# State space preparation: the input matrices' scale ahead of the phase powers, the first C clearing ahead of the input matrices

## The chip, the cores and the metric

One core of a Trainium2 chip runs the whole program. The time is the device time of one execution in microseconds (us). Before the change it was 1484.26 us, the median of three runs (1483.49 to 1489.04).

## The reference

The reference is a small network for one sequence of 256 positions with 1024 channels, in float32. A first block has two layers; each is a mixer (gated linear attention, a short convolution and causal latent attention side by side) followed by a cross attention to 256 memory positions. A second block follows with feed-forwards, a state space mixer (S5) in its first layer and a sparse attention in its second.

The change touches what is computed from the state space mixer's parameters alone. For each of 64 groups with 64 states and 16 channels:

```python
dt = exp(log_dt); mag = exp(a_re * dt)
ab = mag * (cos(a_im * dt) + i sin(a_im * dt))      # one step's factor
z  = (ab - 1) / a                                    # scale of the input matrices
bb = z * b                                           # input matrices, complex
# bu = u @ bb;  state = ab * state + bu;  y = state @ c   along the sequence
```

The kernel treats four positions at once, so it also needs powers of ab, and a table of rotations (the phase of ab taken to 4, 8, 16 and so on) with which the recurrence is run.

## The kernel before, in words

Activations lie transposed, channels on the partitions. Each weight is split into a high part (a copy by ACT, L156) and a remainder (a subtraction by DVE, L157), and each product is three matmuls (L72 is the line of all matmuls, L76 that of all transposes). Weights arrive in halves of 512 KB through SP's queue into `raw`, and the parts into `hi` (three buffers) and `lo` (two). A projection of 256 columns is 48 matmuls of 128x256.

The framework orders the instructions of PE, ACT and DVE before the run, by the order in which the program gives them out and by when it thinks their inputs are ready; on the chip each engine then takes its list in order. POOL is an exception: its instructions are kept exactly in the order of the program (L60 is the line of all of them). Besides the state space work POOL computes the power -1/2 of each norm: `rx` in the cross attention, `rg` in the mixer, `rf` in the final norm.

The preparation `s5_prep` is a generator, and so is `s5_prep_tile`, which makes the records of one of eight tiles (`kt`). The main program calls `bg()` after most of its steps. `bg()` adds to an account a share of PE's time since the last call (0.4 in the first block, 0.7 in the feed-forwards, at most 10000 in all, by prices in the code) and runs the generator from `yield` to `yield` while the account is positive. A step costs POOL's time by the code's prices, but at least 1000. The preparation starts when the first layer's cross attention is about to begin; the tiles go on through the second layer and the first feed-forward. What is left is drained before the state space mixer.

The order of the preparation, as it stands:

- the parameters are loaded into a buffer with the tag `pcb` and transposed by PE; ACT and DVE compute mag, cos and sin, and the powers `pw` of ab;
- `E`: the phase squared over and over, six times, on DVE (44 small instructions with `r4`, in two steps);
- the scale z (`zr`, `zi`): 13 small instructions on DVE;
- `bb`: six products of 128x512 on POOL;
- then for each tile: clear the C tile, again with the tag `pcb` (one buffer); two products each for X0 and X1 from `bb` and `pw`, with sums into `pX`; PE transposes C and ACT copies it into `pcb` (L1256, L1257); POOL's products of C and `pw`; records transposed by PE, copied by ACT (L1279) and stored by POOL's queue; and last the rotation table from `E` on POOL.

In the cross attention (`cross`) the order is: values of the memory (`mem_v(0)`), first queries (`queries(0)`), the squares of hT and their sums (L350) for the norm, `rx`, second queries, scores (DVE's L865 to L872, ACT's L868), and the rest. The functions of the change, and what calls them:

Of the kernel before, what the change touches and what calls it, by code (L numbers as in the profile page):

```python
# [11 lines left out]
F32 = mybir.dt.float32  # L12
# [7 lines left out]
P = 128  # L20
# [8 lines left out]
MUL, ADD, SUB, MAX, MIN = ALU.mult, ALU.add, ALU.subtract, ALU.max, ALU.min  # L29
# [49 lines left out]
class Net:  # L79
# [1028 lines left out]
    def s5_prep(self):  # L1108
        nc, T = self.nc, self.T
        V, A, G, PE = nc.vector, nc.scalar, self.G, self.PE  # L1110
        H = 32
# [4 lines left out]
        v = {n: prm[:, i, :] for i, n in enumerate(names)}  # L1116
        pw = self.pz.tile([P, 2, 5, H], F32, name="pw", tag="pw", bufs=1)
# [15 lines left out]
        p = self.ps("pq")[:, :4 * H].rearrange("p (i q) -> p i q", i=4)  # L1133
# [4 lines left out]
        TT = lambda o, a, b, op: V.tensor_tensor(o, a, b, op=op)  # L1138
# [14 lines left out]

        def cmul(o, a, b, s, E=TT):
            E(o[0], a[0], b[0], MUL)
            E(s[0], a[1], b[1], MUL)
            E(o[1], a[0], b[1], MUL)
            E(s[1], a[1], b[0], MUL)
            E(o[0], o[0], s[0], SUB)
            E(o[1], o[1], s[1], ADD)  # L1160

        pwj = lambda j: (pw[:, 0, j, :], pw[:, 1, j, :])
        tmp = (v["t0"], v["t1"])
        for j, a, b in ((2, 1, 1), (3, 2, 1), (4, 2, 2)):
            cmul(pwj(j), pwj(a), pwj(b), tmp)
        u1, u2 = (v["cos"], v["sin"]), (v["u2r"], v["u2i"])
        cmul(u2, u1, u1, tmp)
        yield

        E = self.pz.tile([P, 6, 3, H], F32, name="E", tag="E", bufs=1)  # L1170
        cmul((E[:, 0, 0], E[:, 0, 2]), u2, u2, tmp)
        for k in range(6):
            if k:
                cmul((E[:, k, 0], E[:, k, 2]), *2 * ((E[:, k - 1, 0], E[:, k - 1, 2]),), tmp)
            V.tensor_scalar(E[:, k, 1], E[:, k, 2], -1.0, None, op0=MUL)
            if k == 3:
                yield
        self.r4 = self.const([P, H], "r4")
        TT(self.r4, v["mag"], v["mag"], MUL)
        TT(self.r4, self.r4, self.r4, MUL)  # L1180

        TT(v["t0"], v["are"], v["are"], MUL)
        TT(v["t1"], v["aim"], v["aim"], MUL)
        TT(v["t0"], v["t0"], v["t1"], ADD)
# [9 lines left out]
        TT(v["zi"], v["zi"], v["dt"], MUL)  # L1194
        yield

        bb = self.pz.tile([P, 2, 512], F32, name="bb", tag="bb", bufs=1)
        GT = lambda o, a, b, op: G.tensor_tensor(o, a, b, op=op)
        zb = [v[n][:, :, None].to_broadcast([P, H, 16]) for n in ("zr", "zi")]
# [2 lines left out]
        cmul([h16(bb[:, i, :]) for i in range(2)], [h16(t) for t in bn], zb,  # L1202
             [h16(s_) for s_ in sc], GT)
        yield
        for kt in range(KD):
            yield from self.s5_prep_tile(kt, v, pw, bb, E)

    def s5_c(self, kt):

# [5 lines left out]
                                       self.T[n][0, 8 * kt:8 * kt + 8].rearrange("g h p -> (g h) p")[:, None, :].to_broadcast([P, 2, 64]))  # L1215
                self.raws.append(raw)

    def s5_prep_tile(self, kt, v, pw, bb, E):
        nc, T = self.nc, self.T
        V, A, G, PE = nc.vector, nc.scalar, self.G, self.PE  # L1220
        dst = self.stash[kt]
# [5 lines left out]
        v4 = lambda t: t.rearrange("p (q i c) -> p q i c", q=4, i=4)  # L1227
        half = (slice(0, 64), slice(64, 128))
        raws = self.raws
        cb = self.pt("pcb", 1).rearrange("p (a q g h) -> p a q g h", a=4, q=4, g=2)  # L1230
        G.memset(cb[:, 0:2], 0.0)
        yield

        b4 = [bb[:, i, q0 * 16:(q0 + 4) * 16].rearrange("p (q h) -> p q h", h=16)[:, :, None, :].to_broadcast(qih)
              for i in range(2)]
# [14 lines left out]
        for c in range(2):  # L1250
            p = self.ps("pq")[:, :P]
            PE.transpose(p, raws[c], self.ident)
            p = p.rearrange("p (q g h) -> p q g h", q=4, g=2)
# [21 lines left out]
        for c in range(2):  # L1275
            p = self.ps("pq")
# [748 lines left out]
```

## Time and profile before

| what | us |
|---|---|
| median of three runs | 1484.26 |
| lowest, highest | 1483.49, 1489.04 |
| the profiled execution | 1480.56 |
| its span, first to last instruction | 1478.7 |
| PE busy | 1418.3 |
| DVE busy | 1010.4 |
| ACT busy | 749.0 |
| POOL busy | 296.5 |

The profile is of one execution. Busy is the time in which an engine had an instruction at work; the rest of the span it waited. PE's ends are modelled, so a busy PE need not be at its peak. The granted clock of PE is 1.00 at its higher level (2.4 GHz) and 0.50 at its lower (1.2 GHz). Times in the views count from the start of the span.

### The profile page before, as it was taken

How to read it: one execution, taken by the hardware profiler on the slowest of the kernel's cores; microseconds unless marked ns; L12 is line 12 of the kernel's file. 1: busy time of each engine (PE TensorE's matmuls, PEld its weight loads, DVE VectorE, ACT ScalarE, POOL GpSimd, SP SyncE). 2: the span in 40 equal slices, each digit the busy share in tenths (PEclk: the TensorE clock that was granted, in tenths of full speed). 3: DMA queues.
4: the chain of work that ended last, by engine and by line, in shares of the span. 5: the costliest groups of instructions: out<-in, count | busy, mean ns of one | idle time of the engine just before them, and what ended most of it. 6: DMA issues, size and time to landing. Idle time of an engine off the chain costs nothing.

```text
span 1478.7 us, 29034 instructions
## 1 busy us (share of the span) xinstructions
PE 1418.3 (96%) x11775; PEld 1326.5 (90%) x11775; DVE 1010.4 (68%) x1815; ACT 749.0 (51%) x1289; POOL 296.5 (20%) x421
## 2 busy tenths in 40 slices
PE   8899979999998999999899999999999989999998
PEld 6898968888988999989799999899999977899987
DVE  6867946887758887648866765566665478657654
ACT  6744555654555554432354444464444377644432
POOL 3000171652627888500000000011000010000000
PEclk9999999999999999996999999999999999999999
DMA  6653633554644766686446556756665631255653
GB/s 189 166 158 101 195 115 108 162 156 131 216 134 144 224 219 198 217 301 219 159 143 194 186 177 187 202 170 181 194 190 188 199 115 58 77 168 185 196 186 131
DMA packets 244296, 252.77 MB, mean 171 GB/s; under 512 B 31378, under 2 KB 226808, under 8 KB 243265
## 3 DMA queue, kind: packets, MB, share of 16 engines
q1 hardware_dynamic: 239408, 236.20, 51.4%
q0 software_dynamic: 4464, 14.63, 3.0%
q8 instruction: 93, 1.52, 0.4%
q14 instruction: 43, 0.34, 0.1%
q10 hardware_dynamic: 288, 0.07, 0.0%
HBM read 235.40 MB, written 15.47 MB: 170 GB/s over the span
## 4 chain that ended last, share of the span: by engine, by line
PE 43%; issue 10%; DVE 3%; POOL 1%; ACT 1%; DMA 0%; POOLq 0%; DVEq 0%; ACTq 0%
PE ps L72 39%; PE pb L72 2%; PE pq L72 1%; DVE lo L157 1%; POOL hq L60 0%; POOL pv L60 0%; DMA raw<-in_w_o_dram 0%; DVE rz L1468 0%; ACT hi L156 0%; POOL pt L60 0%; DVE hqm L1540 0%; PE po L72 0%; DVE ra L1467 0%; DVE s L1805 0%; DVE ra L1457 0%
## 5 line engine op out<-in xcount | busy, mean ns | idle before, releaser
L156 ACT ACTIVATE hi<-raw 128x1024 fp32r<-128x1024 f32 (+3 forms) x428 | 429.9, 1012 | 505.4 <-PE ps L72 198.3
L157 DVE TENSOR_TENSOR lo<-raw,hi 128x1024 fp32r<-128x1024 f32 (+3 forms) x428 | 507.8, 1203 | 104.2 <-issue 51.6
L72 PE MATMUL ps<-xh,hi 128*128 128x256 f32 x1848 | 523.7, 283 | 1.5 <-ACT xh L389 1.1
L72 PE MATMUL ps<-xh,lo 128*128 128x256 f32 x1848 | 520.5, 282 | 3.5 <-DVE lo L157 3.5
L72 PE MATMUL ps<-xl,hi 128*128 128x256 f32 x1848 | 520.8, 282 | 0.6 <-DVE xl L390 0.6
L72 PEld LDWEIGHTS ps<-xh,hi 128*128 128x128 f32 x1848 | 349.1, 189 | 10.2 <-issue 6.3
L72 PEld LDWEIGHTS ps<-xh,lo 128*128 128x128 f32 x1848 | 349.2, 189 | 5.8 <-DVE lo L157 4.2
L72 PEld LDWEIGHTS ps<-xl,hi 128*128 128x128 f32 x1848 | 349.2, 189 | 4.2 <-issue 2.5
L72 PE MATMUL ps<-gl,hi 128*128 128x256 f32 x576 | 162.6, 283 | 1.4 <-DVE gl L1488 1.4
L72 PE MATMUL ps<-gh,hi 128*128 128x256 f32 x576 | 161.7, 283 | 0.9 <-ACT gh L1487 0.9
L72 PE MATMUL ps<-gh,lo 128*128 128x256 f32 x576 | 162.1, 282 | 0.0
L72 PEld LDWEIGHTS ps<-gl,hi 128*128 128x128 f32 x576 | 109.4, 190 | 2.3 <-DVE gl L1488 1.6
L72 PEld LDWEIGHTS ps<-gh,hi 128*128 128x128 f32 x576 | 108.7, 190 | 2.1 <-ACT gh L1487 1.3
L72 PEld LDWEIGHTS ps<-gh,lo 128*128 128x128 f32 x576 | 109.4, 190 | 0.3
L1041 DVE TENSOR_TENSOR ab<-ps,rbf 128x512 f32<-128x512 f32 x66 | 45.6, 690 | 72.8 <-PE ps L72 67.4
L72 PE MATMUL ps<-L,hi 128*128 128x256 f32 (+1 forms) x384 | 72.9, 286 | 0.8 <-ACT L L887 0.8
L72 PEld LDWEIGHTS ps<-L,hi 128*128 128x128 f32 (+1 forms) x384 | 58.4, 182 | 2.0 <-ACT L L887 1.5
L72 PE MATMUL ps<-L,lo 128*128 128x256 f32 (+1 forms) x192 | 54.3, 284 | 1.4 <-DVE bc L732 1.4
L236 DVE TENSOR_TENSOR gl<-e,gh 128x512 fp32r<-128x512 f32 x44 | 32.3, 735 | 29.3 <-ACT gh L235 29.3
L60 POOL TENSOR_TENSOR rkvs<-rkvsa,mhalf 128x2 f32<-128x2 f32 x1 | 0.7, 697 | 190.2 <-DVE rkvsa L369 190.2
L1047 DVE SCALAR_TENSOR_TENSOR e<-e,ab 128x512 f32<-128x512 f32 x44 | 32.6, 741 | 7.4 <-ACT e L1046 7.2
L72 PEld LDWEIGHTS ps<-L,lo 128*128 128x128 f32 (+1 forms) x192 | 35.0, 182 | 2.2 <-DVE bc L732 1.7
(578 smaller groups left out, 2375.3 us busy)
## 6 DMA issues: line engine op xcount, KB each, us to landing
raw<-in_ffn_w_in_dram SPq DMA_DIRECT2D x176, 512.0 KB, 4.3
raw<-in_ffn_w_out_dram SPq DMA_DIRECT2D x68, 512.0 KB, 4.5
raw<-in_w_in_dram SPq DMA_DIRECT2D x24, 512.0 KB, 5.2
stash<-pv POOLq DMA_DIRECT2D x24, 512.0 KB, 4.2
raw<-in_ffn_w_out_dram SPq DMA_DIRECT2D x24, 384.0 KB, 3.5
raw<-in_w_out_dram SPq DMA_DIRECT2D x16, 512.0 KB, 4.2
raw<-in_w_in_dram SPq DMA_DIRECT2D x24, 256.0 KB, 3.4
rec<-stash SPq DMA_DIRECT2D x4, 1536.0 KB, 6.3
```

The source lines that it names most:

```text
L60: return self.tc.keep_in_program_order(f(out, *a, **k))
L72: return self.engine.matmul(out, w, x, **k)
L156: self.nc.scalar.activation(dst(h), src(raw), AF.Copy)
L157: (engine or self.nc.vector).tensor_tensor(dst(l), src(raw), dst(h).bitcast(F32), op=SUB)
L236: self.nc.vector.tensor_tensor(lo, src, hi.bitcast(F32), op=SUB)
L1041: V.tensor_tensor(v[-1], p, rb2, op=MUL)
L1047: V.scalar_tensor_tensor(th, th, 1.0, v[0], op0=ADD, op1=MUL)
```

## The change

Three things move. In `s5_prep` the 13 instructions of the scale come ahead of the phase powers `E` and `r4`. The first tile's C buffer is taken and cleared, by a new function `s5_cb`, before the products `bb` are given out, and handed to `s5_prep_tile`. The phase powers follow the products, in two steps with a `yield` behind them. For the other seven tiles the clearing stays at the head of the tile, but the `yield` behind it is gone, so that it forms one step with the first products.

```diff
@@ s5_prep @@
         cmul(u2, u1, u1, tmp)
         yield
-        E = ...; cmul(...); six squarings with a yield after the fourth; r4
         TT(v["t0"], v["are"], v["are"], MUL)
...
         TT(v["zi"], v["zi"], v["dt"], MUL)
         yield
+        cb = self.s5_cb()
         bb = self.pz.tile([P, 2, 512], F32, name="bb", tag="bb", bufs=1)
...
         yield
+        E = self.pz.tile([P, 6, 3, H], F32, name="E", tag="E", bufs=1)
+        cmul((E[:, 0, 0], E[:, 0, 2]), u2, u2, tmp)
+        for k in range(6):
+            if k:
+                cmul((E[:, k, 0], E[:, k, 2]), *2 * ((E[:, k - 1, 0], E[:, k - 1, 2]),), tmp)
+            V.tensor_scalar(E[:, k, 1], E[:, k, 2], -1.0, None, op0=MUL)
+            if k == 3:
+                yield
+        self.r4 = self.const([P, H], "r4")
+        TT(self.r4, v["mag"], v["mag"], MUL)
+        TT(self.r4, self.r4, self.r4, MUL)
+        yield
         for kt in range(KD):
-            yield from self.s5_prep_tile(kt, v, pw, bb, E)
+            yield from self.s5_prep_tile(kt, v, pw, bb, E, self.s5_cb() if kt else cb)

+    def s5_cb(self):
+        cb = self.pt("pcb", 1).rearrange("p (a q g h) -> p a q g h", a=4, q=4, g=2)
+        self.G.memset(cb[:, 0:2], 0.0)
+        return cb

@@ s5_prep_tile @@
-        cb = self.pt("pcb", 1).rearrange("p (a q g h) -> p a q g h", a=4, q=4, g=2)
-        G.memset(cb[:, 0:2], 0.0)
-        yield
```

## Rows read from the trace of the kernel before

**Rows 1.** The page, busy time and share of the span by engine.
```profile
PE 1418.3 (96%) x11775; PEld 1326.5 (90%) x11775; DVE 1010.4 (68%) x1815; ACT 749.0 (51%) x1289; POOL 296.5 (20%) x421
```
**Rows 2.** By stretch: length, busy PE, PEld, DVE, ACT, POOL, clock, DMA share, GB/s.
```profile
172.00:176.00 4.00, 4.00 (x36) 4.00 (x35) 4.00 (x19) 1.86 (x3) 0.00 (x0) 1.00 0.53 161
...
194.00:197.00 3.00, 3.00 (x15) 3.00 (x16) 0.00 (x0) 1.33 (x2) 2.80 (x5) 0.55 0.02 5
```
**Rows 3.** Timeline of POOL: start, us, engine, line, operation, idle time before.
```profile
180.63 1.06 POOL L60 TENSOR_TENSOR bb<-pX,prm 128x512 f32<-128x512 f32 x1 [49.78 <-DVE prm L1138]
...
189.48 0.31 POOL L60 MEMSET pcb<- 128x256 f32 x1
...
190.22 1.24 POOL L60 TENSOR_TENSOR pt<-bb,pw 128x256 f32<-128x256 f32 x2
...
198.94 1.52 POOL L60 TENSOR_TENSOR pv<-pt 64x256 f32<-64x256 f32 x2
200.54 0.71 POOL L60 TENSOR_TENSOR rx<-rxa,mhalf 128x2 f32<-128x2 f32 x1
```
**Rows 4.** Timeline of ACT, first layer's cross attention.
```profile
179.30 0.83 ACT L843 ACTIVATE qT<-ps,rm 128x256 f32<-128x256 f32 x2
...
189.82 0.22 ACT L1256 ACTIVATE pcb<-pq 64x64 f32<-64x64 f32 x1 [7.99 <-POOL pcb L60]
...
191.70 1.14 ACT L350 ACTIVATE sq<-hT 128x512 f32<-128x512 f32 x2
```
**Rows 5.** Timeline of PE, first layer's cross attention.
```profile
182.39 0.64 PE L72 MATMUL pb<-sq,ones 128*32 128x256 f32 x8
...
192.37 1.58 PE L72 MATMUL pb<-sq,ones 128*32 128x256 f32 x8 [7.73 <-ACT sq L350]
...
200.80 1.89 PE L72 MATMUL pb<-kT,L 128*128 128x256 f32 x8
...
208.57 1.13 PE L72 MATMUL pb<-kT,L 128*128 128x256 f32 x4 [2.05 <-ACT sg L868]
```
**Rows 6.** Timeline of DVE, from the squarings to the first products.
```profile
164.64 0.19 DVE L1138 TENSOR_TENSOR E<-prm 128x32 f32<-128x32 f32 x1
...
175.83 1.21 DVE L157 TENSOR_TENSOR lo<-raw,hi 128x1024 fp32r<-128x1024 f32 x1
...
177.05 0.41 DVE L1138 TENSOR_TENSOR prm<-prm 128x32 f32<-128x32 f32 x2
...
180.36 1.60 DVE L1138 TENSOR_TENSOR prm<-prm 128x32 f32<-128x32 f32 x4
182.55 3.63 DVE L157 TENSOR_TENSOR lo<-raw,hi 128x1024 fp32r<-128x1024 f32 x2 [0.59 <-PE ps L72]
```
**Rows 7.** DVE by line and shape, in 143–181 and 501–541: busy, mean ns.
```profile
L157 DVE TENSOR_TENSOR lo<-raw,hi 128x1024 fp32r<-128x1024 f32 x14 | 17.0, 1217 | 0.0
...
L157 DVE TENSOR_TENSOR lo<-raw,hi 128x1024 fp32r<-128x1024 f32 x14 | 20.8, 1487 | 0.0
```
**Rows 8.** Timeline of ACT, second layer's cross attention.
```profile
403.94 0.82 ACT L843 ACTIVATE qT<-ps,rm 128x256 f32<-128x256 f32 x2
```
**Rows 9.** Timeline of PE, second layer's cross attention.
```profile
416.30 1.89 PE L72 MATMUL pb<-kT,L 128*128 128x256 f32 x8
```
**Rows 10.** Timeline of POOL, second layer's cross attention.
```profile
413.73 0.72 POOL L60 TENSOR_TENSOR rx<-rxa,mhalf 128x2 f32<-128x2 f32 x1 [7.44 <-DVE rxa L369]
...
418.34 2.03 POOL L60 TENSOR_TENSOR pt<-pcb,pw 128x256 f32<-128x256 f32 x2 [2.98 <-ACT pcb L1257]
```
**Rows 11.** Timelines of POOL and of PE in the feed-forward, tiles 6 and 7.
```profile
550.05 2.76 POOL L60 TENSOR_TENSOR pX<-pt 64x256 f32<-64x256 f32 x2
...
552.24 1.27 PE L76 MATMUL pq<-ident,pX 128*128 128x128 f32 x8
...
590.31 2.76 POOL L60 TENSOR_TENSOR pX<-pt 64x256 f32<-64x256 f32 x2
...
605.95 1.04 PE L76 MATMUL pq<-ident,pX 128*128 128x128 f32 x8
```

More of the change, by code (lines that the diff above doesn't have):

```diff
@@ L1168, in s5_prep @@
         yield
[L1170 to L1176, printed above, removed]
-                yield
-        self.r4 = self.const([P, H], "r4")
-        TT(self.r4, v["mag"], v["mag"], MUL)
-        TT(self.r4, self.r4, self.r4, MUL)
         TT(v["t0"], v["are"], v["are"], MUL)
@@ L1216, in s5_c, with s5_prep_tile @@
                 self.raws.append(raw)
-    def s5_prep_tile(self, kt, v, pw, bb, E):
+    def s5_cb(self):
+        cb = self.pt("pcb", 1).rearrange("p (a q g h) -> p a q g h", a=4, q=4, g=2)
+        self.G.memset(cb[:, 0:2], 0.0)
+        return cb
+    def s5_prep_tile(self, kt, v, pw, bb, E, cb):
         nc, T = self.nc, self.T
@@ L1229, in s5_prep_tile @@
         raws = self.raws
-        cb = self.pt("pcb", 1).rearrange("p (a q g h) -> p a q g h", a=4, q=4, g=2)
-        G.memset(cb[:, 0:2], 0.0)
-        yield
         b4 = [bb[:, i, q0 * 16:(q0 + 4) * 16].rearrange("p (q h) -> p q h", h=16)[:, :, None, :].to_broadcast(qih)
```

## The prediction

> **What bounds the kernel now.** I read the page's busy table and its slices first, then the table of busy times by stretch around the changed lines, then who waits for whom there, then each engine in order of time. The busy table says that PE works 96% of the span [rows 1]: time can only be had where PE stands still or runs at the lower clock. The table by stretch shows such a hole where the changed code runs, in the first layer's cross attention: in 172–176 us PE and DVE are both full and POOL rests, in 194–197 PE works at a granted clock of 0.55, while DVE rests and POOL is full [rows 2].
>
> The timelines say why. POOL, which runs in the order written, starts the six products of the input matrices at 180.63, when DVE has delivered their factors, and clears the C tile (pcb) only behind them, at 189.48 [rows 3]. ACT takes its instructions in order too: its first copy into pcb waits 7.99 us for that clearing, and the squares of hT, which have nothing to do with the state space, stand behind it and run at 191.70 [rows 4]. PE needs these squares and has stood still for 7.73 us when it gets them, at 192.37 [rows 5]. A second string hangs on the same queue: the power of the norm (rx) is a POOL instruction behind all of tile 0's work so far, so it runs at 200.54 [rows 3], and the scores of heads 2 and 3, at 208.57, come 2.05 us after PE is ready for them [rows 5].
>
> **The change part by part.**
>
> *The clearing ahead of the products.* The same 0.31 us memset now stands before the six products, on a POOL that was idle for 49.78 us before them [rows 3]. What it must wait for, the transposes of the parameters out of the same buffer, is long done. It costs nothing there. It takes away ACT's wait, so the squares run when the copy of the first queries allows, and PE's 7.73 us go. In the pause the clock fell, too: eight square-sum matmuls take 0.64 us at 182.39 and 1.58 us at 192.37 [rows 5], 0.94 more, and in 194–197 fifteen instructions take 3.00 us where, at 36 in 4 us (0.111 us each), 27 would fit [rows 2], 1.3 more: 2.2 us. The squares will not be ready at once: ACT has pcb's eight copies and the queries' copy before them; I leave 0.3 us of waiting. PE's string gains 7.7 + 2.2 − 0.3 = 9.6 us.
>
> *The scale ahead of the phase powers.* On DVE 44 small instructions (six squarings of six, six negations, two for r4) stood before the 13 of the scale; now the 13 come first. The squarings began at 164.64 and the scale at 177.05 [rows 6]; the first product followed 180.63 − 177.05 = 3.6 us later. In the squarings' place it follows at 164.6 + 3.6 = 168.2, 12.4 us earlier. The phase powers lose nothing: their first reader is tile 0's rotation table, which POOL reaches after rx. The DVE work is the same.
>
> What is late next is DVE. It was idle during most of the products; at 168–184 it is full, and the two engines slow each other: DVE's 128x1024 remainder (L157) takes 1.217 us while POOL rests and 1.487 us in a stretch of dense POOL work [rows 7]. Beside the first products it lost more: two L157 at 3.63 us instead of 2.43, and four small ones at 1.60 us [rows 6] instead of 0.8: 2.0 of 5.6 us, or 36%. At that rate the second half of the queries' weights, ready at 175.83 + 1.22 = 177.05 [rows 6], comes 0.36 × 8.8 = 3.2 us later. PE's 48 matmuls on these weights end at 182.39 [rows 5], so it takes up the second half 24 × 0.111 = 2.7 us before, at 179.7: a stall of 0.5 us. Bounds: none, and 6.2 us, if DVE loses all of the 8.8 us. I take the 0.5 of the nearest rows. PE's string: −9.1 us.
>
> POOL is slowed as well. From the first product to tile 0's last sum ahead of rx it took 198.94 + 1.52 − 180.63 = 19.8 us [rows 3], mostly beside an idle DVE. From 168.2 that ends at 188.0. Beside a full DVE a pair of 256-wide products takes up to 2.03 us [rows 10], alone 1.24 [rows 3]: 0.8 more, and of some ten pairs I let half be hit: 4 us, less 0.3 for the clearing: rx at 191.7, bounds 187.7 and 196. That is 8.8 us before 200.54.
>
> *Where the strings meet.* The scores at 208.57 need both. PE's own string would be there at 208.57 − 2.05 − 9.1 = 197.4, rx's at 208.57 − 8.8 = 199.8. The later decides: **−8.8 us**, between −4.5 (rx at 196) and −11.2. An independent measure agrees: the second layer's cross attention is the same code without the blocked clearing. From its ACT copy at 403.94 to its eight score matmuls at 416.30 are 12.4 us [rows 8, 9]; in the first layer from 179.30 to 200.80 are 21.5 us [rows 4, 5]: 9.1 us apart.
>
> The rows on L157 show contention at 22%, not a full block. The Trainium skill, "SBUF — State Buffer", section "Who interferes with whom", says that a DVE instruction with two SBUF inputs contends with a GpSimd instruction that reads SBUF, through a lock held for the whole instruction, and not with one that only writes. By that, DVE would stand for all of POOL's reading: the first rival below.
>
> *The steps that are handed out differently.* `bg()` gives out steps by prices in the code, and a step with little POOL work is charged 1000. From tile 1 on, clearing (230) and first products (1792) are one step of 2022 instead of two charged 2792. Replaying the charges: the order of tile 0's work against rx does not change; the phase powers come two calls later; from tile 1 on each tile runs up to one call ahead of before. Two places follow. In the second cross attention tile 3's step with the C products now stands before rx on POOL instead of behind it: those products waited 2.98 us for ACT's pcb copies, until 418.34, and took 2.03 us, while rx ran at 413.73 [rows 10]. If the copies stay where they are, rx comes 6.6 us late; if ACT makes them in the earlier step, before the squares, they cost ACT some 1.4 us there and spare it as much later. I take 0, the latter, bounds 0 and +6.6. In the feed-forward, PE's transposes of tile 6 begin at 552.24, while POOL's last sum for them, begun at 550.05, still runs [rows 11]; handed out earlier they could make PE wait. I take 0: POOL gains there too, since tile 3's last step now precedes the final norm's powers. With that cover gone it is the third rival.
>
> **Sum.** −8.8 us. The profiled execution took 1480.56 us (span 1478.7), 3.7 us below the median of the runs shown, so against itself it gives 1471.8; against the median 1484.26 − 8.8 = **1475.5 us**.
>
> **The rivals.**
> 1. *DVE is blocked whenever POOL reads.* PE stalls 6.2 us in the first queries and the clock falls as before (2.2 us): PE's string gains 9.6 − 8.4 = 1.2 us, and the time is 1484.26 − 1.2 = 1483.1. For: small ones beside the products took twice their time. Against: L157's 22%. Chance 0.13.
> 2. *The pause only moves*, or the change doesn't do what it says. The C copies need PE's transposes, handed out one call later, behind the first values product; if ACT's copies wait there for PE, or if DVE is not given the scale first, rx stays near 200 and half of the gain is lost: 1480–1484. For: ACT's order is fixed in advance. Against: PE is not late there, and the second layer makes the same copies without such a wait. Chance 0.17.
> 3. *Slower than before: PE's tile work overtakes POOL.* PE runs in order, and one call is a chunk of 48 matmuls, 48 × 0.111 = 5.3 us. In the feed-forward PE's transposes begin 4.4, 4.9, 0 and 12.9 us after POOL's sums of tiles 4, 5, 6 and 7 (for the last two [rows 11]). Tiles 4 to 6 pulled ahead by one call each stall 0.9 + 0.4 + 5.3 us; tile 7's move from behind the first output block (132 matmuls) to ahead of the last inner chunk, 14.7 + 5.3 = 20 us, and stall 7.1. With one clock drop of 2.2 that is 15.9 us: 1484.26 − 8.8 + 15.9 = 1491.4. It decides from 8.8 us of such waits. Against: POOL starts tile 4 earlier too, and whoever orders PE can leave a transpose until its input is due. Chance 0.10.
>
> **How the numbers follow.** My case, 0.60, has its own range of 1471 to 1480. About what a measurement of this kernel can tell from no change is 0.5%, or 7.4 us: faster by more means under 1476.8, slower over 1491.7. The line is 1.3 us above my time, and the second layer's 9.1 us and the bound of −11.2 lie on its lower side, so I put 0.44 of the 0.60 there, and 0.04 for a gain beyond the bounds by shorter waits later, from rival 2's share. Rivals 1 and 2 count as the same, rival 3 as half slower, with 0.02 for a worse one. So faster 0.48, same 0.45, slower 0.07. The range of 1469 to 1486 holds my case and the first two rivals and leaves out the third.
>
> **What would show it.** Right: ACT's first pcb copy without a wait for POOL; the products starting near 168; rx before 194; no granted clock near 0.5 at 190; the stretch of 21.5 us near 12.5. Wrong: L157 at 165–182 well over 1.5 us with PE waiting for `lo`; the second layer's rx behind the C products; more waits of PE for tile copies after 463. If the hole closes and the time does not move, the third rival has it.

## The result, and the profile after

The changed kernel takes 1497.80 us (median of six runs, 1495.81 to 1503.44); the kernel before, on the same chip, 1484.38 (1483.49 to 1489.04). The ratio is 1.0074, 95% interval [1.0050, 1.0098]: 0.7% slower. Forecast were 1475.5, within 1469 to 1486, and only 0.07 for slower. The prediction was wrong.

The profiled execution took 1497.42 us, its span is 1495.6 (before 1478.7). PE does the same 11775 matmuls and is busy longer [rows 1]; its mean granted clock is 0.976 where it was 0.984:

```profile
PE 1431.0 (96%) x11775; PEld 1338.7 (90%) x11775; DVE 1013.9 (68%) x1815; ACT 749.1 (50%) x1289; POOL 294.4 (20%) x421
```

To find the place I took the starts of six POOL powers that both kernels have, and cut the span there: `rg` of the first layer, `rx`, `rq` of the second layer's mixer, `rx` of the second layer, `rf`, and the power `rs` of the state space mixer. The rows after, by stretch (length, busy PE, PEld, DVE, ACT, POOL, clock, DMA share, GB/s):

```profile
129.89:201.75 71.86, 63.26 (x488) 59.73 (x487) 58.76 (x164) 33.24 (x59) 25.52 (x23) 0.93 0.43 137
201.75:259.14 57.39, 54.67 (x423) 48.48 (x422) 36.85 (x80) 34.34 (x71) 12.78 (x28) 1.00 0.43 125
259.14:422.50 163.36, 155.17 (x1204) 144.69 (x1203) 120.34 (x208) 88.04 (x170) 74.09 (x112) 0.97 0.51 160
422.50:465.36 42.86, 42.39 (x342) 38.26 (x341) 29.29 (x64) 27.07 (x54) 14.92 (x31) 1.00 0.49 157
465.36:676.97 211.61, 198.68 (x1675) 194.18 (x1673) 141.74 (x180) 94.16 (x149) 131.26 (x178) 0.97 0.63 206
```

Before, the five lengths are 71.33, 57.24, 155.95, 45.18 and 202.52 us, and the clocks 0.95, 1.00, 0.99, 1.00 and 0.99. So the stretch of the first cross attention, which was to lose 8.8 us, is 0.5 longer; the second layer up to its `rx` is 7.4 longer, of which the next stretch gives 2.3 back; the feed-forward with the final norm is 9.1 longer. (The 17 us of the spans are these five, 0.7 ahead of them and 1.4 behind. The medians are only 13.4 us apart: the profiled execution before is 3.8 us below the median of its kernel, the one after lies at it.) Of the feed-forward's, clock accounts for some 4 us (0.97 of 211.61 against 0.99 of 202.52 us, as far as two digits carry) and PE's standing for the rest.

**The first cross attention after.** Four engines in order of time (start, us, engine, line, operation, idle before). First POOL, which answers to [rows 3]:

```profile
143.00 0.31 POOL L60 MEMSET pcb<- 128x256 f32 x1 [11.47 <-PE pq L76]
169.75 1.37 POOL L60 TENSOR_TENSOR bb<-pX,prm 128x512 f32<-128x512 f32 x1 [26.43 <-DVE prm L1138]
171.74 2.12 POOL L60 TENSOR_TENSOR pv<-pX,prm 128x512 f32<-128x512 f32 x1 [0.62 <-DVE prm L1138]
173.81 1.06 POOL L60 TENSOR_TENSOR bb<-pX,prm 128x512 f32<-128x512 f32 x1
174.83 1.06 POOL L60 TENSOR_TENSOR pv<-pX,prm 128x512 f32<-128x512 f32 x1
...
201.75 0.72 POOL L60 TENSOR_TENSOR rx<-rxa,mhalf 128x2 f32<-128x2 f32 x1 [7.16 <-DVE rxa L369]
```

DVE, which answers to [rows 6]:

```profile
171.68 1.21 DVE L157 TENSOR_TENSOR lo<-raw,hi 128x1024 fp32r<-128x1024 f32 x1
172.82 1.08 DVE L1138 TENSOR_TENSOR E<-E,prm 128x32 f32<-128x32 f32 x1
173.93 0.99 DVE L1138 TENSOR_TENSOR E<-E 128x32 f32<-128x32 f32 x1
174.84 1.10 DVE L1138 TENSOR_TENSOR prm<-E 128x32 f32<-128x32 f32 x1
175.86 1.31 DVE L1138 TENSOR_TENSOR E<-E 128x32 f32<-128x32 f32 x1
177.10 1.31 DVE L1138 TENSOR_TENSOR prm<-E 128x32 f32<-128x32 f32 x1
...
178.65 0.68 DVE L229 TENSOR_TENSOR hT<-ps,hT 128x512 f32<-128x512 f32 x1
...
180.84 1.21 DVE L157 TENSOR_TENSOR lo<-raw,hi 128x1024 fp32r<-128x1024 f32 x1
```

ACT and PE, which answer to [rows 4] and [rows 5]:

```profile
179.37 0.91 ACT L389 ACTIVATE xh<-hT,gt 128x256 fp32r<-128x256 f32 x2 [5.24 <-DVE hT L229]
...
185.65 1.06 ACT L156 ACTIVATE hi<-raw 128x1024 fp32r<-128x1024 f32 x1 [4.43 <-DMA raw<-in_mem_wv_dram]
...
187.33 0.21 ACT L1260 ACTIVATE pcb<-pq 64x64 f32<-64x64 f32 x1
...
194.37 1.06 ACT L156 ACTIVATE hi<-raw 128x1024 fp32r<-128x1024 f32 x1 [3.63 <-DMA raw<-in_mem_wo_dram]
...
195.94 1.14 ACT L350 ACTIVATE sq<-hT 128x512 f32<-128x512 f32 x2
```

```profile
182.11 0.58 PE L72 MATMUL ps<-xh,lo 128*128 128x256 f32 x1 [4.33 <-DVE lo L157]
...
196.62 0.63 PE L72 MATMUL pb<-sq,ones 128*32 128x256 f32 x4 [4.27 <-ACT sq L350]
...
204.99 1.89 PE L72 MATMUL pb<-kT,L 128*128 128x256 f32 x8
```

The first steps happened as forecast: the clearing at 143.00, the products from 169.75 (forecast 168.2), ACT's first copy into pcb without a wait for POOL. Then DVE's and POOL's rows have to be read side by side. An instruction of the squarings, which takes 0.18 or 0.19 us alone [rows 6], takes 1.08 from 172.82, and so ends at 173.90; POOL's product from 171.74 ends at 173.86. The next ends at 174.92 and the product beside it at 174.87; the third at 175.94, the product at 175.89. Each of the three lasts until a POOL product is over. The other way round, the 128x1024 remainder begun at 171.68, 0.06 us ahead of a product, takes its usual 1.21 us, and it is the product that takes 2.12 instead of 1.06. In these rows the one that comes second waits for all of the first. The Trainium skill, "SBUF — State Buffer", section "Who interferes with whom", says that a DVE instruction with two SBUF inputs, as all of these have, contends with a GpSimd instruction that reads SBUF, and that the ports they share are an exclusive lock. This trace agrees, with these ends 0.04 to 0.05 us apart.

The addition to hT stands behind these squarings on DVE: 178.65, where DVE before did it at 171.91. From there it spreads: ACT's `xh` waits 5.24 us, the remainder L157 is late and PE stands 4.33 us, the raw buffers come free late, so that one part of the weights reaches ACT 4.43 us after ACT is ready and a later one 3.63 us. The squares stand behind both, run at 195.94, and PE stands another 4.27 us. One hole of 7.73 us has become two of 8.60 together, with a granted clock of 0.50 behind the first of them (182.2 to 187.0), and `rx` waits for its input (7.16 us) and no longer for POOL's work.

**The second layer after.** Of its 7.4 us, 2.4 lie ahead of the mixer's `rg` and 5.1 between `rg` and `rx`. There PE waits 3.38 us for a copy of ACT (`asT`, the transposed attention weights) where it waited 1.96 before, and the granted clock of the 10 us around it is 0.66; before it was 1.00 (357 to 367). First the row before, then the rows after:

```profile
360.69 0.86 PE L72 MATMUL po<-asT,mv 128*64 128x256 f32 x4 [1.96 <-ACT asT L625]
...
365.55 1.54 PE L72 MATMUL po<-asT,mv 128*64 128x256 f32 x4 [3.38 <-ACT asT L625]
...
362.00:372.00 10.00, 6.62 (x31) 5.73 (x30) 6.08 (x13) 5.08 (x9) 0.00 (x0) 0.66 0.27 88
...
422.50 0.73 POOL L60 TENSOR_TENSOR rx<-rxa,mhalf 128x2 f32<-128x2 f32 x1 [3.45 <-DVE rxa L369]
```

`rx` itself has POOL waiting 3.45 us for its input, so the C products, which are now ahead of it, do not hold it up. What makes `asT` late I did not trace.

**The feed-forward after.** PE, at the transposes of tile 6, which began without a wait in [rows 11]:

```profile
559.36 1.12 PE L76 MATMUL pq<-ident,pX 128*128 128x128 f32 x4 [4.47 <-POOL pX L60]
```

### The profile page after: what moved, and what is told of

Its sections match the earlier page's. It is cut to its first block, busy times and chain, and to the rows that moved or that the text cites. A ratio compares the mean times of both kernels' runs of the same rounds, so it can differ in the third digit from the quotient of the medians.

```text
span 1495.6 us, 29029 instructions
## 1 busy us (share of the span) xinstructions
PE 1431.0 (96%) x11775; PEld 1338.7 (90%) x11775; DVE 1013.9 (68%) x1815; ACT 749.1 (50%) x1289; POOL 294.4 (20%) x421
## 4 chain that ended last, share of the span: by engine, by line
PE 65%; issue 12%; DVE 8%; POOL 7%; DMA 4%; ACT 3%; SPq 0%; POOLq 0%; DVEq 0%; ACTq 0%
PE ps L72 55%; PE pb L72 5%; POOL pv L60 3%; DVE lo L157 3%; POOL pt L60 2%; PE pq L72 2%; PE po L72 1%; POOL pX L60 1%; PE pb L76 1%; DMA stash<-pv 1%; DMA memn<-in_mem_dram 1%; DMA raw<-in_w_out_dram 1%; ACT hi L156 1%; DMA recw<-stash 1%; DMA raw<-in_w_in_dram 0%
## 5 line engine op out<-in xcount | busy, mean ns | idle before, releaser
L157 DVE TENSOR_TENSOR lo<-raw,hi 128x1024 fp32r<-128x1024 f32 (+3 forms) x428 | 503.0, 1193 | 112.9 <-issue 61.7
L235 ACT ACTIVATE gh<-e 128x512 fp32r<-128x512 f32 x44 | 27.3, 620 | 22.7 <-DVE e L1048 22.7
```

The costliest lines, as they stand in the source:

```text
L157: (engine or self.nc.vector).tensor_tensor(dst(l), src(raw), dst(h).bitcast(F32), op=SUB)
L235: self.nc.scalar.activation(hi, src, AF.Copy)
```

## The experiments

The first theory (T1): two separate losses. In the first cross attention the gain is eaten by the squarings beside POOL's products; and the merged step from tile 1 on changes the hand-out, which costs the later 14 us. Rivals: R1, that any other order at the start costs the same; R2, that the merged step is the whole loss.

The ratios are to the kernel before, run on the same chip between the runs of the experiment. Its median on these chips was 1487.7 to 1490.5 us, 3 to 6 above that of the profiled chip, so stretches of two traces are compared for what is well over 1 us, and the times by ratio alone. (The five differences of x5, for example, add up to 6.7 us, while its ratio makes 2.7.)

| run | ratio | 95% interval |
|---|---|---|
| x1 changed, own step for each clearing | 1.0040 | 1.0020 to 1.0059 |
| x2 before, merged step alone | 1.0061 | 1.0041 to 1.0081 |
| x3 before, early clearing alone | 1.0044 | 1.0027 to 1.0061 |
| x4 as x1, phase powers given out late | 1.0029 | 1.0012 to 1.0045 |
| x5 as x1, account exactly as before | 1.0018 | 0.9997 to 1.0039 |
| x6 as x3, account exactly as before | 1.0008 | 0.9987 to 1.0029 |
| x7 before, 230 taken from the account | 1.0030 | 1.0010 to 1.0051 |
| x8 before, `rx` ahead of tile 0 | 0.9990 | 0.9971 to 1.0010 |
| x9 as x8, transposes of X held too | 0.9995 | 0.9976 to 1.0015 |
| x10 as x5, phase powers on POOL | 0.9963 | 0.9944 to 0.9983 |
| x11 as x10, `rx` ahead of the C product | 0.9911 | 0.9893 to 0.9930 |
| x12 changed, phase powers on POOL | 0.9996 | 0.9975 to 1.0016 |

The lengths of the five stretches above, less those of the trace before (us):

| run | rg to rx | to rq | to rx, layer 2 | to rf | to rs |
|---|---|---|---|---|---|
| changed | +0.5 | +0.2 | +7.4 | −2.3 | +9.1 |
| x1 | +0.5 | +0.7 | +6.9 | +0.5 | +2.2 |
| x2 | +1.0 | +1.7 | +3.6 | −2.4 | +8.5 |
| x3 | +0.3 | +0.4 | +4.8 | +0.5 | +1.2 |
| x4 | +0.2 | +1.6 | +7.6 | +0.7 | +2.2 |
| x5 | +1.0 | +1.7 | +2.7 | +0.8 | +0.5 |
| x6 | +0.4 | +2.6 | +1.7 | +1.0 | +0.5 |
| x7 | +0.2 | −0.5 | +7.2 | +0.6 | +0.8 |
| x8 | −10.7 | +7.8 | +0.7 | +1.0 | −0.3 |
| x9 | −10.8 | +9.8 | +6.0 | +0.7 | −0.4 |
| x10 | −6.8 | +2.0 | +1.6 | +0.6 | −0.9 |
| x11 | −10.2 | +2.3 | +2.1 | +1.7 | +1.4 |
| x12 | −7.7 | −1.4 | +4.6 | −2.4 | +7.2 |

**x1, the changed kernel with a step of its own for each clearing.**

```diff
         raws = self.raws
+        if kt:
+            yield
```

> The changed kernel, but the clearing of C of tiles 1 to 7 is a step of its own again (a yield behind it), so that the account pays as many steps as before. Three theories of the 13.4 us that were lost. T1 (two separate causes): the merged step lets the preparation run ahead of its old place and costs about 14 us between 250 us and 700 us; the scale ahead of E gives nothing at the first cross attention, because its gain of some 9 us is lost again where E's small instructions stand beside POOL's products. T1 expects 1484 to 1487 us, `rx` of the first cross attention near 201.7 us as in the changed kernel, and the feed-forwards' `rf` about 215 us before the first record of the state space mixer, as before. R1 (the displaced order at the start alone shifts everything behind it, the hand-out is innocent): 1493 us or more. R2 (the merged step is the whole loss, and the first cross attention did gain): 1475 to 1479 us.

The feed-forward's loss fell from 9.1 to 2.2 us, as T1 has it, but the ratio is 1.0040 and the second layer still loses 6.9. Neither T1 nor R2; the median of 1493.36 us is in R1's range, though the kernel before was 4 us slower on this chip too (1488.44).

**x2, the merged step alone.**

```diff
         G.memset(cb[:, 0:2], 0.0)
-        yield
+        if not kt:
+            yield
```

> The kernel before, but the yield behind the clearing of C is gone for tiles 1 to 7: the hand-out of the changed kernel with the old order of scale, E, products and first clearing. T1 expects the hand-out's loss by itself, 1494 to 1500 us, with the first cross attention as before (PE's gap of 7.7 us at 192 us and `rx` at 200.5 us both there) and new gaps of PE in the second layer and the first feed-forward. R1 expects the time of before, 1483 to 1486 us.

1.0061 (1495.52 us), with the first cross attention as before: T1's number, and R1 falls as the whole story, since the order at the start is the old one here. The loss is in the feed-forward. PE waits there for tile copies of ACT (2.89 us before) and, where it did not wait before, for POOL's sums of tile 6. The two rows are x2's:

```profile
480.11 1.08 PE L72 MATMUL pq<-pX,pcb 128*32 128x128 f32 x16 [4.59 <-ACT pv L1280]
...
555.77 1.12 PE L76 MATMUL pq<-ident,pX 128*128 128x128 f32 x4 [3.47 <-POOL pX L60]
```

**x3, the early clearing alone.**

```diff
+        cb = self.s5_cb()
         bb = self.pz.tile(...)
...
-        G.memset(cb[:, 0:2], 0.0)
         yield
```

> The kernel before, but the first tile's C buffer is cleared ahead of the products bb; E stays ahead of the scale, and every step keeps its price (an empty step stands where the first clearing was). ACT's copies into the C buffer no longer stand behind bb, and E is done before bb begins. T1 expects PE's gap of 7.7 us at 192 us to go, as ACT's squares come some 8 us earlier, but `rx` to stay behind POOL's work for the first tile at about 200 us, so that PE stands some us ahead of the scores instead: 1479 to 1485 us. The prediction's own view (the wait of ACT for the clearing is the whole hole, `rx` comes when the squares come) would give 1475 to 1478 us.

The hole at 192 us went and `rx` stayed behind POOL, both as expected, but the time came out at 1.0044, over the range: again the second layer, +4.8 us. x1 and x3 have one thing in common that I had overlooked. A step is charged what POOL's instructions in it are priced at, or 1000; given out with bb, the clearing made that step 230 dearer. By a replay of the charges, in the kernel before the account of a later call is positive by 88 when it decides on tile 0's C transposes; less 230 they fall to the next call, and all that follows with them.

**x4, the phase powers given out inside tile 0.**

```diff
+            if not kt:
+                yield from self.phases()     # E and r4, behind the C products
```

> The changed kernel with a step of its own for each clearing (as x1), and the phase powers E and r4 given out in two steps inside the first tile, behind the C products, instead of beside bb: no squaring stands beside POOL's products. If the squarings' waits for POOL's reads ate the gain of the first cross attention (T1), hT's addition comes 5 us earlier than in x1, PE's gaps near 182 us (4.3) and 196 us (4.3) close, `rx` comes by 194 to 197 us, and the time is 1473 to 1480 us. If the gain was lost in another way (the PE order, the place of ACT's copies), it is within 2 us of x1.

1.0029, not the gain that T1 expected, but this does not tell what it was meant to tell. Giving the steps out later did not move them on DVE: the squarings still stood from 172.51 us on beside bb, and several of their instructions took 1.1 us each. And with two steps fewer ahead, tile 0's second C product moved in front of `rx`.

**x5 to x7, the account.** The new theory T2: the hand-out's account alone makes the later losses, the 230 in x1 and x3 and the merged step in the changed kernel. x5 is x1, and x6 is x3, with the clearing in the step before bb, where it costs nothing more; POOL's list then differs from before in that one place. x7 is the kernel before with one line:

```diff
+        self.owed -= 230
         yield
         for kt in range(KD):
```

> The changed kernel with the hand-out of the kernel before to the last unit: the clearings of tiles 1 to 7 are steps of their own, and the first clearing is given out in the scale's step, which pays its 1000 anyway, instead of in the step of bb, which it made 230 dearer. POOL's list then differs from before in the place of one clearing only. In x1, x3 and x4, which all carried these 230, the second layer's `rg` came 14 to 16 us late on POOL and the layer lost 5 to 8 us. T2 (the account is what costs: 230 for the second layer, the merged step for the feed-forward): the second layer's loss goes, only the first cross attention is left, within 2 us of before (ratio 0.999 to 1.002). R1 (any other order at the start costs what x1 and x3 lost): ratio 1.003 or more, as x1. In the first cross attention E stands beside bb, as in the changed kernel: hT's addition some 7 us late, PE's gap of 4 us near 182 us still there.

> x3 (the clearing early alone, E ahead of the scale and done before bb begins), with the clearing given out in the step before bb, so that the account is that of before. T2: the second layer as before; the hole at 192 us goes but `rx` stays behind POOL's first tile near 200 us, so the time is within 2 us of before (ratio 0.998 to 1.001). R1: ratio 1.003 or more, as x3. Against x5 it tells what the squarings beside POOL's products cost: if that is much, x6 is 3 us or more below x5; by x3 against x1 (1.0044 and 1.0040) it is nothing in the end, because POOL's first tile sets `rx` either way.

> The kernel before, instruction for instruction, but 230 more taken from the account once, behind bb; nothing is added or removed. T2: this alone puts the first tiles' steps a call later and loses the second layer's 4 to 6 us, as x1 and x3: ratio 1.003 to 1.004, `rg` of the second layer 11 us or more later. R1 (the loss belongs to the displaced order at the start, not to the account): ratio 0.999 to 1.001.

T2 holds for the 230: x7 adds and removes no instruction and loses 0.3%; the loss sits in the second layer, +7.2 us (+2.7 in x5, +1.7 in x6). By the times alone x5 and x7 can't be told apart, as their intervals overlap; the place of the loss in the traces does it. In both kernels POOL waits for ACT's copies before tile 2's C product, but in the kernel before that product starts at 342.82, in x7 at 356.08. The mixer's norm `rg` stands behind it: its input is ready at 352.05, and it runs at 360.45 (348.18 before):

```profile
351.88 0.17 DVE L369 TENSOR_SCALAR rga<-gms 128x8 f32<-128x8 f32 x1
...
356.08 1.82 POOL L60 TENSOR_TENSOR pt<-pcb,pw 128x256 f32<-128x256 f32 x2 [21.26 <-ACT pcb L1258]
...
360.45 1.66 POOL L60 TENSOR_TENSOR rg<-rga,mhalf 128x8 f32<-128x8 f32 x1
```

With the old account the intervals of x5 and x6 take in 1. In both the first cross attention gains nothing, for opposite reasons. In x5 DVE is blocked, as in the changed kernel:

```profile
182.60 0.58 PE L72 MATMUL ps<-xh,lo 128*128 128x256 f32 x1 [3.94 <-DVE lo L157]
...
197.37 1.07 PE L72 MATMUL pb<-sq,ones 128*32 128x256 f32 x4 [3.98 <-ACT sq L350]
```

In x6, where E is done before bb begins, the squares come early and `rx` is still at 201.00, because POOL begins bb at 181.38 and has tile 0 ahead of `rx`; PE stands at the transposes of X and ahead of the scores instead:

```profile
197.06 1.11 PE L76 MATMUL pq<-ident,pX 128*128 128x128 f32 x4 [2.30 <-POOL pX L60]
...
209.03 2.07 PE L72 MATMUL pb<-kT,L 128*128 128x256 f32 x4 [4.14 <-ACT sg L868]
```

**x8 and x9, `rx` ahead of tile 0.** The account is held (and paid later) until `rx` is given out; in x9 held again from the second C product to mem_v(1).

```diff
+        while self.owed > 0 and not self.hold:      # in bg()
...
+        self.hold, self.cap = True, 20000           # behind bb
...
         r = self.rpow(self.sumsq(self.hT, KD, "pb"), D, 2, "rx")
+        self.hold = False
```

> The kernel before, with one thing held back: the steps of the first tile are given out only behind the power `rx` of the first cross attention (the account keeps what it is owed meanwhile, so from the next call on the hand-out is that of before). POOL then does bb, `rx`, and the first tile; ACT's copies into the C buffer no longer stand ahead of its squares, and the scale and E stay in their old order. If POOL's chain of bb and the first tile ahead of `rx` is what the first cross attention really waits for (so that neither the clearing nor the scale could gain alone), `rx` comes at 190 to 193 us instead of 200.5, and the time falls by 5 to 9 us: ratio 0.994 to 0.997. If PE's stand only moves behind `rx` (the first tile's transposes, mem_v(1)), the ratio is 0.998 to 1.001.

> x8 moved `rx` from 200.5 to 191.3 us, but PE then stood 2.1 and 2.8 us at the transposes of the first tile's X, which stood in its list ahead of what it could have done, and only some 3 us of the 10 were left at the next norm (245 us). Here the account is held a second time, behind the first tile's second C product, until mem_v(1): the transposes of X are given out behind the scores instead of between them. If the place of these transposes is what kept the rest, PE's two gaps near 196 and 199 us go, with the lower clock behind them, the norm at 245 us comes 6 to 9 us early and the ratio is 0.993 to 0.996. If the gap moves on once more (the transposes wait at their new place, or ACT's evictions of them push mem_v(1)), the ratio is 0.998 to 1.001, as x8.

In x8 `rx` came at 191.30, and 7.8 of the 10.7 us were lost again by the next norms: PE, in order, waits for POOL at the transposes of X, which are now late.

```profile
197.41 0.66 PE L76 MATMUL pq<-ident,pX 128*128 128x128 f32 x4 [2.07 <-POOL pX L60]
...
200.87 1.11 PE L76 MATMUL pq<-ident,pX 128*128 128x128 f32 x4 [2.81 <-POOL pX L60]
```

x9 took these two waits away and found others a little further on, 2.09 us for ACT and 3.81 us for DVE's softmax sums. Both ratios are those expected if the gap only moves on. With bb from 181 us on, neither of the two places that I tried for tile 0's work was free.

**x10 and x11, no small DVE work beside the products.** In x10, POOL computes E and r4 in tile 0's last step, when it has nothing urgent:

```diff
-        E = ...; cmul(...) ... V.tensor_scalar(...); r4 by TT
+        def phases():
+            cmul(..., tmp, GT); ...; G.tensor_scalar(E[:, k, 1], E[:, k, 2], -1.0, None, op0=MUL)
...
+        if not kt:
+            self.phases()
         G.memset(fr[:, 0, :, 0:1], 1.0)
```

> x5 (scale first, clearing early, account as before), but the phase powers E and r4 are computed by POOL in the first tile's last step, just ahead of the rotation table, and DVE has none of the 44 small instructions (the two empty steps keep the price). This is the prediction's case without its contention: bb starts near 170 us and nothing small of DVE stands beside it. If DVE's waits behind POOL's reads ate the gain of the first cross attention (T1, the first rival of the prediction), hT's addition comes 6 to 7 us earlier than in x5, PE's gap of 4 us near 180 us goes, `rx` comes at 191 to 195 us, and the ratio is 0.994 to 0.997. If the gain is lost without contention too (POOL's first tile ahead of `rx`, PE's waits for X), the ratio is 0.998 to 1.002.

0.9963, and the first theory's point is shown: x5 and x10 differ in the engine and the place of these instructions alone, and their intervals do not touch. Not told apart is how much of it is DVE's waiting and how much the instructions' own work, since x10 takes both off DVE. hT's addition is at 172.62 us (178.54 in x5), PE's wait near 180 is gone, `rx` is at 194.74:

```profile
172.62 0.68 DVE L229 TENSOR_TENSOR hT<-ps,hT 128x512 f32<-128x512 f32 x1
173.22 3.70 DVE L157 TENSOR_TENSOR lo<-raw,hi 128x1024 fp32r<-128x1024 f32 x2
```

The two remainders take 3.70 us where 2.43 is usual; contention is still there, and the large instructions behind them take long too (up to 3.90 for two remainders), but the forty small ones are not among them.

x11 adds x8's hold, set behind tile 0's C transposes, so that POOL does `rx` between the sums of X and the first C product.

> x10 with one more thing: the account is held behind the first tile's C transposes until `rx` is given out, so that POOL does `rx` between the X sums and the first C product (in x10 `rx` was ready at 191.2 us and waited for the C product until 194.7). If POOL's C product is the last thing ahead of the scores, `rx` comes 3 us earlier than in x10 and the time falls by 2 to 4 us more: ratio to the kernel before 0.993 to 0.996. If what follows (second queries, scores, PE's waits for ACT) takes its place, it is the ratio of x10, 0.995 to 0.998.

0.9911, faster than both kernels: by the ratio 13 us below the kernel before (11.3 between the medians), more than expected.

```profile
191.16 0.71 POOL L60 TENSOR_TENSOR rx<-rxa,mhalf 128x2 f32<-128x2 f32 x1 [0.69 <-DVE rxa L371]
```

```profile
130.07:191.16 61.09, 59.23 (x488) 56.30 (x487) 48.59 (x120) 33.27 (x59) 22.22 (x18) 1.00 0.52 162
```

The stretch up to `rx` is 61.09 us at clock 1.00, against 71.33 at 0.95. Against x10, PE's wait at the scores of heads 2 and 3 falls from 2.50 to 0.61 us and the next norm is 3.3 us earlier; the ratios are 0.5% apart, some 8 us, on different chips. The two traces do not show this: over all five stretches x11's is not shorter than x10's (−2.7 and −3.5 us). What makes up the 8 us stays open.

**x12, the changed kernel with that one edit** (the diff of x10, on the changed kernel).

> The changed kernel with one edit: the phase powers on POOL, as in x10; the merged step and the 230 of the first clearing stay. If the two losses are separate (the contention at the first cross attention, worth 0.55% by x5 against x10, and the merged step, 0.6% by x2), only the first is healed: ratio to the kernel before 1.001 to 1.004 (1.0074 less 0.0055), `rx` of the first cross attention at 194 to 197 us, and the feed-forward still 8 to 9 us longer between `rf` and the state space mixer's first record. If the early order heals the later loss too (everything behind starts earlier and in step), the ratio is 0.995 to 0.998, as x10.

0.9996, just under the range for separate losses: the first cross attention is healed (−7.7 us, `rx` at 192.86), the feed-forward still loses 7.2, a little less than expected, and PE waits for tile 6 as in the changed kernel:

```profile
544.88 1.12 PE L76 MATMUL pq<-ident,pX 128*128 128x128 f32 x4 [3.30 <-POOL pX L60]
```

x12 is 0.33% above x10, x2 0.61% above the kernel before. These are two estimates of what the merged step costs, each with an interval of ±0.2% or more.

## Why the prediction was wrong

- *The hole and its cause: right.* ACT's wait for the clearing went and the products began within 1.6 us of the forecast. x10, in which POOL has the forecast's order up to `rx`, has it at 194.74, forecast 191.7 within 187.7 and 196. That x11 has it at 191.16 is luck for the forecast: there the C product, which the forecast counted ahead of `rx`, is behind it.
- *Contention on DVE, "0.5 us, bounds none and 6.2": the first failing step.* I took a rate (36%) from a few rows and spread it over time. The trace after shows a price by instruction: a 128x32 instruction of the squarings that meets a POOL product waits it out, 1.06 us beside bb. Sixteen of the forty that read or write E took over 0.5 us, and the forty kept DVE busy for 14.40 us where it was 5.19, so DVE ran 6.7 us late at hT's addition (0.7 of it from ahead of the stretch). In place of 0.5 us PE stood 4.33 us in the first queries. I had 44 such instructions in hand and priced only the two large ones of the queries' weights. The remainder's 22% [rows 7], my argument against a full block, is no argument: for an instruction of 1.2 us one wait is a small share, for one of 0.18 us it is five times its time.
- *What hangs on DVE there: missed.* I followed the delay to PE's second half of the queries, not to hT, ACT's `xh`, the raw buffers and the next weights. So I let the squares run "when the copy of the first queries allows", and they came 4.2 us later than before. My 0.3 us of waiting for them was 4.27.
- *The hand-out, "I take 0": the second failing step, and the larger.* By x2 the merged step costs 0.61%, some 9 us. The places I had named were partly right: PE overtook POOL at tile 6, by 4.47 us (my third rival had 5.3), and the lower clock followed. But the second layer's `rx` did not wait for the C products, and what I had not looked at, the end of the second layer's mixer, lost 5.1 us. The replay itself stopped too early: I found that tile 0 stays ahead of or behind `rx` as before, and did not see the margin of 88 at its C transposes, which the 230 use up (x7). In the changed kernel, which has both, `rg` is 3.7 us late as in x2, not 12 to 15 as in x1 and x7: the merged step hides what the 230 do alone.
- *The rivals.* The first named the mechanism of the first cross attention and gave it 0.13; the third that of the feed-forward, at 0.10, on top of the full gain. What happened is both at once: x5's 0.18% (its interval takes in 0) and x2's 0.61% make 0.79, measured 0.74. I had treated them as excluding each other.
- *The independent measure* (the second layer's 9.1 us shorter stretch) was near what could be had (6.8 us in x10, 10.2 in x11) and said nothing on whether this change would get it.

## What to carry to other kernels

Price contention by the instruction: count the small two-input DVE instructions that will stand beside POOL's products. Each of them can wait out a whole product, and here sixteen of forty waited long. When work is handed out by an account, replay it to the last call and list the smallest margins first; here a merged step cost 0.61% and 230 units charged in another step 0.30%, as much as the stall that the edit was to remove (8.8 us, 0.6%) and half of it. An edit that frees one engine pays only if the next one in line is free too: clearing early (x6), and with it scale early (x5), gained nothing; with the phase powers off DVE as well (x10) they gained 0.37%. The phase powers off DVE alone were not run.

## What was not expected of the hardware

- Negations of E, a 128x32 operation on DVE with a single input, were held up in the traces too: 1.09 us beside a POOL product in x4, 0.17 alone.
- In x10 POOL mostly takes 0.23 to 0.25 us for a 128x32 product that takes DVE 0.18. All of E and r4 took it 12.5 us (205.41 to 217.93), and from 190 to 222 us PE waits for no POOL instruction: the slower engine was the better one.
- Waits of about equal length did not have one price. PE's wait for tile 4's copy is 2.89 us before and 2.95 after; only after the second did the granted clock fall to 0.50 (484.3 to 487.3 us).
